# Index key gathers in pairs behind row conversions, and small 32-column products joined to page visits, in a one-core decoder-layer kernel

## The chip, the cores and the metric

The kernel runs on one core of a Trainium2 chip. The metric is the device time of one execution in microseconds (us), lower is better. The engines are TensorE (PE, with its weight loads as PEld), VectorE (DVE), ScalarE (ACT), GpSimd (POOL) and SyncE (SP), which issues most transfers. Each engine works through its own instructions in the order in which they were written; semaphores hold it back until its inputs are there.

## What is computed

One layer of a hybrid decoder, for 256 prompt tokens and 8 requests of 8 new tokens each (320 columns in all), with three groups of heads that read the same projection:

```
z = x @ w_in                        # 2048 -> 8272, split among the three groups
A: I[t,s] = sum_h w[t,h] relu(q_idx[t,h] . k_idx[s])   # 16 index heads x 64
   keep the top 256 (prompt: 64) keys of each query, softmax attention over them
   # 8 heads x 128; keys of the new tokens' requests: 16 pages x 128 past keys + 8 new
B: f = lb + (1-lb) sigmoid(bf);  S_t = diag(f_t) S_{t-1} + (1-f_t) outer i_t
   o_t = S_t^T q_t                  # 4 heads, RMSNorm per head
M: attention into 256 memory tokens # 4 heads
y = LayerNorm(alpha*x + [A*silu, B*silu, M*silu] @ w_out)
```

The keys and values of the past lie in pages of 128 keys that a page table names. The index keys too: `cache_idx_k[page_table]`.

## The kernel before

All products are done in float32 quality. A weight block of 1024 columns comes into `wr`, ACT casts each half to a rounded part `wh`, DVE or POOL subtracts to get the remainder `wl`, and PE multiplies three times (`xh*wh`, `xl*wh`, `xh*wl`). These projection matmuls write `pj`, 48 to a block of 128 output columns, and are most of PE's work. Rotary embedding and evacuation of `pj` are DVE's, POOL's and ACT's.

The order on each engine is fixed when the program is built. A class `Plan` keeps an estimated clock for each engine and an estimated time at which each tile is ready. The main loop issues, at the planned time, either a quantum of projection matmuls (6 of them) or a page unit; around each it resumes the generators in the list `bg` (`background`). A generator yields `need(tiles, ps=n)`: it goes on when the planned clock has passed the tiles' planned times and `n` PSUM banks are free. On the chip nothing of these times is left, only the order.

The parts that matter here:
- **Page units** (`unit`, `units_now`). K units (scores of past keys), V units (their values), XK and XV units (memory of the requests). In these the stationary operand has 32 columns, so four products stand side by side in the array; the trace prints their form as `128*32`. K and V units run in twos where the pages of both are there. A K unit writes half of the bank `kv`, a V unit adds to the bank `va`.
- **Index keys** (`idx_load`). For the four pairs of requests in turn, 16 gathers by POOL fetch the index keys, 128 columns each, into one tile of 2048 columns; their row numbers come from the integer table `poff`.
- **Sample index scores** (`idx_sample`). Twenty steps; in each, `stack` splits 512 (or 8) gathered keys of two requests into rounded part and remainder with ACT and DVE (tile `cat1`), PE takes a group of four score matmuls with the queries (`bp`; the trace says `mA<-cat,bp` or `mB<-cat,bp`), and ACT or DVE applies relu into a ring of four slots of `cat0`. After every second step the head sum (`sums`, matmuls `va<-cat,t`, 32-column form) weighs the heads and is copied or added into the score row `sc` by DVE. The last sums are followed by `topk_sample`: 32 rounds of maximum and replacement on DVE over 1032 scores, then a mask (`maskb`).
- **Prompt index scores** (`idx_prompt`). For each of eight head pairs, four small matmuls once the rotated query `IQ[i]` has been added up, by DVE or POOL, whichever the plan thinks is earlier (`TT`).
- **Sample softmax** (`soft(p)`). Scores of the new tokens (`kv<-akS,qpad`, 32-column form), then mask products (`mA/mB<-maskb,emat`), softmax and transposes for the V units.
- **HGRN** (`hgrn`). For each of four heads a long chain; one piece of it is the product of queries and state (`mA/mB<-bp,t`, 32-column form, 8 matmuls).

## Time and profile before

| | us |
|---|---|
| median of three runs | 907.29 (902.79, 907.29, 907.40) |
| profiled execution | 904.91 |
| its span | 903.2 |
| PE busy | 880.1 (97%) |
| DVE busy | 574.8 (64%) |
| ACT busy | 415.2 (46%) |
| POOL busy | 333.4 (37%) |
| mean granted TensorE clock | 0.996 of full speed |

The profile was taken from one execution. A line gives the start of an instruction from the start of the span, its duration, the engine, the line in the code (nearly all instructions are issued by one helper and have line 142), what it writes and reads, and its form; `x8` is a run of eight alike. In brackets stands how long the engine had been idle, and what ended that. PE's matmuls overlap, so the step from one start to the next tells more than a duration. Plain float32 matmuls run in two passes and count twice.

### The profile page before, as it was taken

The numbers are of one execution on the slowest core, as the hardware profiler recorded it, in microseconds if no ns is written. First come the engines' busy times: TensorE is split into PE (matmuls) and PEld (weight loads), VectorE is DVE, ScalarE is ACT, GpSimd is POOL, SyncE is SP. The second block draws the span as 40 slices with busy tenths as digits, with TensorE's granted clock in tenths as the row PEclk, the third lists the DMA queues.
The fourth block names the chain that finished last, engine by engine and source line by source line (L and its number), as shares of the span: only waits on it lengthen the run. The fifth ranks groups of instructions, "written<-read, shape, count | busy, mean of one in ns | idle before, by whom it ended". The sixth has DMA issues, their size and how long they took to land.

```text
span 903.2 us, 18928 instructions
## 1 busy us (share of the span) xinstructions
PE 880.1 (97%) x6615; PEld 738.9 (82%) x6618; DVE 574.8 (64%) x1191; ACT 415.2 (46%) x872; POOL 333.4 (37%) x322
## 2 busy tenths in 40 slices
PE   8999999999999999999999999999999999999995
PEld 7888877898899888788978787877799788788885
DVE  6677998777689973566654653567544332663656
ACT  6434756654454354334364343434455343554432
POOL 0577774236645530252531441253330001133425
PEclk9999999999999999999999999999999999999998
DMA  8555444499899978999999999999974999856532
GB/s 301 159 167 164 149 115 128 140 402 411 326 409 339 388 277 290 393 353 354 386 378 410 375 404 360 406 352 382 376 290 136 377 409 411 320 168 202 190 94 116
DMA packets 80273, 266.62 MB, mean 295 GB/s; under 512 B 10097, under 2 KB 16946, under 8 KB 79538
## 3 DMA queue, kind: packets, MB, share of 16 engines
q1 hardware_dynamic: 78130, 261.22, 78.2%
q0 software_dynamic: 2048, 4.20, 1.6%
q8 instruction: 52, 0.85, 0.4%
q14 instruction: 43, 0.35, 0.1%
HBM read 256.65 MB, written 8.73 MB: 294 GB/s over the span
## 4 chain that ended last, share of the span: by engine, by line
PE 85%; DVE 10%; DMA 2%; issue 1%; ACT 1%; SPq 0%; POOL 0%; ACTq 0%; DVEq 0%; POOLq 0%
PE pj L142 48%; PE mB L142 12%; PE mA L142 9%; PE va L142 9%; PE kv L142 6%; DVE PT L142 4%; DVE t L142 2%; DVE wl L142 1%; DVE cat L142 1%; DMA wr<-in_wt 1%; DMA pg<-in_xT 1%; ACT wh L142 1%; SPq L142 0%; DVE pg L142 0%; ACT cat L142 0%
## 5 line engine op out<-in xcount | busy, mean ns | idle before, releaser
L142 PE MATMUL pj<-xh,wh 128*128 128x320 f32 x1008 | 324.6, 322 | 1.3 <-ACT t L142 0.9
L142 DVE TENSOR_TENSOR wl<-wr,wh 128x512 fp32r<-128x512 f32 x239 | 186.7, 791 | 212.7 <-ACT wh L142 188.7
L142 PE MATMUL pj<-xh,wl 128*128 128x320 f32 x1008 | 311.0, 309 | 0.8 <-POOL wl L142 0.8
L142 PE MATMUL pj<-xl,wh 128*128 128x320 f32 x1008 | 311.0, 309 | 0.0
L142 ACT CAST wh<-wr 128x512 fp32r<-128x512 f32 x338 | 204.2, 618 | 219.8 <-PE pj L142 170.1
L142 POOL TENSOR_TENSOR wl<-wr,wh 128x512 fp32r<-128x512 f32 x99 | 131.8, 1337 | 334.9 <-ACT wh L142 310.7
L142 PEld LDWEIGHTS pj<-xh,wh 128*128 128x128 f32 x1008 | 189.3, 188 | 28.7 <-issue 22.5
L142 PEld LDWEIGHTS pj<-xl,wh 128*128 128x128 f32 x1008 | 189.4, 188 | 1.2
L142 PEld LDWEIGHTS pj<-xh,wl 128*128 128x128 f32 x1008 | 189.1, 188 | 1.1 <-POOL wl L142 1.1
L142 POOL TENSOR_TENSOR t<-t,t 128x256 fp32r<-128x256 f32 (+4 forms) x69 | 55.6, 807 | 126.2 <-ACT t L142 77.5
L142 ACT ACTIVATE t<-t 128x320 f32<-128x320 f32 (+1 forms) x68 | 29.3, 454 | 66.9 <-DVE t L142 66.2
L142 PE MATMUL kv<-pg,qpad 128*32 128x256 f32 x1024 | 59.8, 381 | 0.0
L142 PE MATMUL va<-pg,PT 128*32 128x512 f32 x512 | 58.7, 596 | 0.0
L142 PEld LDWEIGHTS kv<-pg,qpad 128*32 128x32 f32 x1024 | 31.0, 110 | 21.8 <-issue 1.9
L142 PEld LDWEIGHTS va<-pg,PT 128*32 128x32 f32 x512 | 14.8, 109 | 30.8 <-issue 28.9
L142 DVE MAX8 PT<-PT 128x8 f32<-128x1032 f32 x32 | 39.4, 1232 | 0.5
L142 DVE MATCH_REPLACE8 PT<-PT 128x1032 f32<-128x1032 f32 x32 | 39.0, 1218 | 0.0
L142 POOL DMA_INDIRECT pg<-in_ci,poff x32 | 34.4, 1075 | 11.8 <-issue 8.7
L142 DVE TENSOR_TENSOR t<-t,t 128x320 f32<-128x320 f32 (+4 forms) x55 | 23.0, 418 | 21.9 <-ACT t L142 15.7
L142 POOL DMA_INDIRECT S<-in_ci,poff x32 | 33.4, 1045 | 9.0 <-issue 8.4
L142 POOL TENSOR_TENSOR t<-t,tabm 128x320 f32<-128x320 f32 x16 | 14.0, 876 | 43.6 <-DVE t L142 38.4
L142 PE MATMUL mA<-t,t 128*128 128x64 f32 (+6 forms) x172 | 26.3, 300 | 2.8 <-POOL t L142 2.8
(321 smaller groups left out, 1288.8 us busy)
## 6 DMA issues: line engine op xcount, KB each, us to landing
pg<-in_ck SPq DMA_DIRECT2D x128, 512.0 KB
pg<-in_cv SPq DMA_DIRECT2D x128, 512.0 KB
wr<-in_wt SPq DMA_DIRECT2D x126, 512.0 KB
wr<-in_wo SPq DMA_DIRECT2D x36, 512.0 KB
wr<-in_wm SPq DMA_DIRECT2D x16, 512.0 KB
pg<-in_cXK SPq DMA_DIRECT2D x8, 512.0 KB
pg<-in_cXV SPq DMA_DIRECT2D x8, 512.0 KB
pg<-in_xT SPq DMA_DIRECT2D x8, 320.0 KB
```

Source lines behind the costliest of these rows:

```text
L142: res = f(*a, **k)
```

## The change

- `idx_load` no longer uses an integer table. For each two gathers, DVE converts two columns of row numbers to integers (`row`, a ring of four small tiles), and POOL issues the two gathers that read them. Pairs are at least `PACE` = 2.4 us apart in the plan. The gathers go in the order in which the steps use them, alternating between the two tiles of a side (`sp`), and each quarter of a tile is known by its own planned time.
- `idx_sample` gets a second buffer for relu results (`more`, a page buffer), so that it holds eight slots of 512 and eight of 8, and sums heads four steps at once: four stretches of sums where there were ten. First sums are copied by ACT, not DVE. Score groups need `LAG2` = 0.4 us of planned distance from their inputs, prompt score groups `LAG` = 1.5 us.
- The scores of the new tokens leave `soft` for a generator `new_keys` of their own, and use a bank of the general kind. It and HGRN's query-state product are marked `visit=True`: they wait, for up to `VISIT_WAIT` = 9 us of the plan, until a page unit has been issued, and are then issued right behind it (`join_visit`).
- The two XK units share a bank and go together, as do the two XV units.

In the order on PE, this is the place of the first head sums, before:

```order
L142 MATMUL mA_1273<-cat_4_85,bp_1048 128x512
L142 MATMUL mA_1273<-cat_4_85,bp_1049 128x512
L142 MATMUL mA_1274<-cat_4_85,bp_1048 128x512
L142 MATMUL mA_1274<-cat_4_85,bp_1049 128x512
L142 MATMUL va_1279<-cat_3_84,t_371 32x512 x4
L142 MATMUL pj_1240<-xh,wh_1184 128x320
```

and after, on the same engine (`cat_3` and `pg_1101` are the two buffers of relu results, `t` the head weights):

```order
L146 MATMUL mB_1424<-cat_4_84,bp_1097 128x512
L146 MATMUL mB_1424<-cat_4_84,bp_1098 128x512
L146 MATMUL mB_1425<-cat_4_84,bp_1097 128x512
L146 MATMUL mB_1425<-cat_4_84,bp_1098 128x512
L146 MATMUL va_1430<-cat_3_83,t_372 32x512 x3
L146 MATMUL va_1430<-pg_1101,t_372 32x512 x4
L146 MATMUL va_1430<-cat_3_83,t_372 32x512
L146 MATMUL pj_1391<-xh,wh_1331 128x320
```

Two head sums of four matmuls each have become one stretch of eight, behind the fourth step of scores and not behind the second.

On PE again, the first head's query-state product before (`bp` holds the state, `vN` and `kN` are HGRN's values and keys):

```order
L142 MATMUL kv_5794<-pg_5589,qpad_368 32x256 x2
L142 MATMUL mA_5851<-vN_5196,kN_5784 128x128 x2
L142 MATMUL pj_5718<-xh,wh_5691 128x320
L142 MATMUL pj_5718<-xl,wh_5691 128x320
L142 MATMUL pj_5718<-xh,wl_5692 128x320
L142 MATMUL pj_5718<-xh,wh_5691 128x320
L142 MATMUL pj_5718<-xl,wh_5691 128x320
L142 MATMUL pj_5718<-xh,wl_5692 128x320
L142 MATMUL mB_5885<-bp_5173,t_5000 32x128 x8
L142 MATMUL mB_5894<-t_5171,vN_5196 128x128 x2
```

and after:

```order
L146 MATMUL kv_5898<-pg_5658,qpad_369 32x256 x2
L146 MATMUL kv_5898<-pg_5708,qpad_369 32x256 x2
L146 MATMUL mB_5932<-bp_5165,t_5062 32x128 x8
L146 MATMUL mA_5941<-t_5163,vN_5179 128x128 x2
L146 MATMUL mA_5941<-t_5062,t_5853 128x128
```

The product had a stretch of its own between two pieces of work in full width; now it stands right behind a K unit.

On POOL, the gathers around the first addition of a rotated query (`t<-t,t`), before:

```order
L142 DMA pg_361<-in_ci,poff 128x128 x6
L142 TENSOR_TENSOR t_554<-t_550,t_549 128x256
L142 DMA pg_361<-in_ci,poff 128x128 x8
L142 DMA S_686<-in_ci,poff 128x128 x2
L142 TENSOR_TENSOR t_749<-t_745,t_744 128x256
```

and after:

```order
L146 DMA pg_359<-in_ci,row_446 128x128 x2
L146 DMA S_360<-in_ci,row_491 128x128 x2
L146 DMA S_360<-in_ci,row_523 128x128 x2
L146 TENSOR_TENSOR t_561<-t_557,t_556 128x256
L146 DMA pg_359<-in_ci,row_583 128x128 x2
L146 DMA pg_359<-in_ci,row_615 128x128 x2
```

Each two gathers now read a `row` tile of their own that DVE writes, and the two tiles of a side fill together.

The diff, cut to its core:

```diff
@@ -32,10 +32,14 @@
...
 RES = 7
+PACE = 2.4
 HOMES = 5
...
 SOON = 0.4
+LAG = 1.5
+LAG2 = 0.4
+VISIT_WAIT = 9.0
 TABLES = {AF.Exp: "exp_ln", AF.Ln: "exp_ln", AF.Silu: "silu", AF.Sqrt: "sqrt"}
@@ -205,8 +209,9 @@
...
 
-def need(*aps, ps=1):
-    return (aps, ps)
+def need(*aps, ps=1, lag=0.0, visit=False):
+    return (aps, ps, lag, visit)
 
@@ -672,22 +670,26 @@
...
                               start=False, stop=True)
-                bg.insert(0, [extract(p), ((VACC[p],), 0)])
+                bg.insert(0, [extract(p), need(VACC[p], ps=0)])
                 done.add(("vdone", p))
         elif kind == "XK":
-            ps = PS([128, 256], "kv")
+            if p == 0:
+                st["xk"] = PS([128, 512], "kv")
+            ps = st["xk"][:, 256 * p:256 * p + 256]
             for h in range(4):
...
                               tl[b // 2][:, b % 2, 256 * h:256 * h + 256], start=h == 0, stop=h == 3)
-            bg.insert(0, [xsoft(p, ps), ((ps,), 0)])
+            if p == 1:
+                for g in range(2):
+                    bg.insert(0, [xsoft(g, st["xk"][:, 256 * g:256 * g + 256]), need(st["xk"], ps=0)])
         else:
-            va = PS([128, 512], "va")
+            va = PS([128, 512], ("va", "kv")[p])
             for nt in range(2):
...
                               tl[b // 2][:, b % 2, 512 * nt:512 * nt + 512], start=nt == 0, stop=nt == 1)
-            bg.insert(0, [xextract(p, va), ((va,), 0)])
+            bg.insert(0, [xextract(p, va), need(va, ps=0)])
             if p == 1:
@@ -717,10 +719,12 @@
...
         kind, p, u = punits[n]
-        if kind[0] == "X" or u % 2:
+        if u % 2 or kind[0] == "X" and p:
             return 1
-        if loaded(n + 1) and (kind == "K" or u < 6 or "attn" in done):
+        if loaded(n + 1) and (kind != "V" or u < 6 or "attn" in done):
             return 2
+        if kind[0] == "X":
+            return 0
         if since[0] is None:
@@ -751,16 +755,27 @@
...
     def idx_load():
-        for p in range(4):
-            st["ci", p] = t = new([128, PAST], ("pg", "S")[[0, 1, 0, 1][p]])
-            plan.split.add(t.tensor.name)
-            for j in range(16):
-                if j % 2 == 0:
-                    yield from idle("POOL", 1.5)
-                POOL.indirect_dma_start(out=t[:, 128 * j:128 * j + 128], out_offset=None, in_=I["ci"],
-                                        in_offset=bass.IndirectOffsetOnAxis(ap=poff[:, 16 * p + j:16 * p + j + 1],
-                                                                            axis=0))
-            done.add(("ci", p))
+        t = -9.0
+        for sp in range(2):
+            for p in (2 * sp, 2 * sp + 1):
+                st["ci", p] = x = new([128, PAST], ("pg", "S")[p % 2])
+                plan.split.add(x.tensor.name)
+            for c in range(2):
+                for f in (1, 0):
+                    for p in (2 * sp, 2 * sp + 1):
+                        for j in range(8 * f + 4 * c, 8 * f + 4 * c + 4, 2):
+                            while plan.now < t + PACE:
+                                yield
+                            yield from idle("POOL", 1.5)
+                            t = plan.now
+                            row = new([128, 2], "row", I32)
+                            DVE.tensor_copy(row, st["rows"][:, 16 * p + j:16 * p + j + 2])
+                            for i in range(2):
+                                x = st["ci", p][:, 128 * (j + i):128 * (j + i) + 128]
+                                POOL.indirect_dma_start(out=x, out_offset=None, in_=I["ci"],
+                                                        in_offset=bass.IndirectOffsetOnAxis(ap=row[:, i:i + 1], axis=0))
+                        st["gathered", p, c, f] = x
 
@@ -819,29 +834,44 @@
...
                  for a in range(2)]
-
-        def sums(sp, c, f, r):
-            n = r[0].shape[-1]
-            if f == 1:
-                st["scp"] = PS([128, 512], "va")
-            for g in range(4):
-                PE.matmul(st["scp"][32 * g:32 * g + 32, 0:n], wpad[sp][:, g, f, :], r[g],
-                          start=f == 1, stop=f == 0 or c == 2)
-            if f == 0 or c == 2:
+        more = new([128, 2048], "pg")
+        plan.split.add(more.tensor.name)
+        st["more"] = 1
+        slots = [t[:, 512 * i:512 * i + 512] for t in (early, more) for i in range(4)]
+        small = [early[:, 2784 + 8 * i:2792 + 8 * i] for i in range(8)]
+        used = [0, 0]
+        def relu_slot(n):
+            ring = slots if n > 8 else small
+            used[n > 8] += 1
+            return ring[used[n > 8] % 8][:, 0:n]
+        def sums(sp, rs):
+            for c in sorted({c for c, f in rs}):
+                n = rs[c, 1][0].shape[-1]
+                ps = PS([128, 512], "va") if c < 2 else PS([128, 8])
+                for f in (1, 0) if c < 2 else (1,):
+                    for g in range(4):
+                        PE.matmul(ps[32 * g:32 * g + 32, 0:n], wpad[sp][:, g, f, :], rs[c, f][g],
+                                  start=f == 1, stop=f == 0 or c == 2)
                 d = sc[:, 512 * c:512 * c + n]
-                if sp == 0:
-                    DVE.tensor_copy(d, st["scp"][:, 0:n])
+                if sp:
+                    DVE.tensor_add(d, d, ps[:, 0:n])
+                elif c < 2:
+                    ACT.copy(d, ps[:, 0:n])
                 else:
-                    DVE.tensor_add(d, d, st["scp"][:, 0:n])
+                    DVE.tensor_add(d, ps, tail8)
 
...
                 n, raw = 512, st["ci", 2 * sp + a][:, 1024 * f + 512 * c:1024 * f + 512 * c + 512]
+                kk = [stacked[:, 512 * (2 * (k % 2) + j):512 * (2 * (k % 2) + j) + n] for j in range(2)]
             else:
                 n, raw = 8, st["nk", sp][:, 8 * a:8 * a + 8]
-            kk = [stacked[:, 512 * (2 * (k % 2) + j):512 * (2 * (k % 2) + j) + n] for j in range(2)]
+                kk = [stacked[:, 2048 + 8 * (4 * sp + 2 * a + j):2056 + 8 * (4 * sp + 2 * a + j)] for j in range(2)]
             for j in range(2):
@@ -851,38 +881,44 @@
...
         def keys_in(k):
-            return k >= len(steps) or steps[k][1] == 2 or ("ci", 2 * steps[k][0] + steps[k][3]) in done
+            if k >= len(steps) or steps[k][1] == 2:
+                return True
+            sp, c, f, a = steps[k]
+            x = st.get(("gathered", 2 * sp + a, c, f))
+            return x is not None and plan.avail(x) <= plan.now
 
...
             yield
-        yield need(st["ci", 0])
         kk = stack(0)
-        prev = None
+        rs, full = {}, None
         for k, (sp, c, f, a) in enumerate(steps):
             n = kk[0].shape[-1]
-            yield need(ql, qh, *kk, ps=2)
+            yield need(ql, qh, *kk, ps=2, lag=LAG2)
             pd = [PS([128, 512]), PS([128, 512])]
...
                 PE.matmul(pd[j][:, 0:n], qlr[:, b], kk[j], start=False, stop=True)
-            if a == 0 and k:
-                sums(*prev)
-            r = [relu_slot(n), relu_slot(n)]
-            ACT.activation(r[0], pd[0][:, 0:n], AF.Relu)
-            if plan.t["ACT"] < plan.t["DVE"] + 0.5:
-                ACT.activation(r[1], pd[1][:, 0:n], AF.Relu)
-            else:
-                DVE.tensor_scalar(r[1], pd[1][:, 0:n], 0.0, None, op0=OP.max)
-            prev = (sp, c, f, r if a == 0 else prev[3] + r)
+            if full:
+                sums(*full)
+                full = None
+            r = rs.setdefault((c, f), [])
+            for j in range(2):
+                r.append(relu_slot(n))
+                if j == 0 or plan.t["ACT"] < plan.t["DVE"] + 0.5:
+                    ACT.activation(r[-1], pd[j][:, 0:n], AF.Relu)
+                else:
+                    DVE.tensor_scalar(r[-1], pd[j][:, 0:n], 0.0, None, op0=OP.max)
+            if a == 1 and (c, f) in ((0, 0), (2, 1)):
+                full, rs = (sp, rs), {}
             while not keys_in(k + 1):
...
                 yield
-        yield need(*prev[3], ps=0)
-        sums(*prev)
-        DVE.tensor_add(sc[:, 1024:1032], sc[:, 1024:1032], tail8)
+        yield need(*[x for r in full[1].values() for x in r], ps=1)
+        sums(*full)
+        del st["more"]
         free(ql, qh, *st.pop("wpad"))
@@ -931,7 +967,7 @@
...
             yield from wait(("iq", i))
-            yield need(IQ[i], ik, ps=2)
+            yield need(IQ[i], ik, ps=2, lag=LAG)
             d = [PS([128, 384]), PS([128, 384])]
@@ -1028,23 +1064,28 @@
...
 
-    def soft(p):
-        yield from wait(("K", p), "topk", ("ak", 7), "masks")
-        yield need(akS, st["qpad"], ps=0)
-        while "kv" in st or plan.slot_free("kv", 1) > plan.now:
+    def new_keys(p):
+        yield from wait(("ak", 7))
+        while p not in S:
             yield
-        Sp = S[p]
-        ps = PS([128, NS], "kv")
+        yield need(akS, st["qpad"], visit=True)
+        ps = PS([128, NS])
         for hh in range(2):
...
                               stop=hh == h2 == 1)
-        ACT.activation(Sp[:, PAST:], ps, AF.Copy, scale=QS)
+        ACT.activation(S[p][:, PAST:], ps, AF.Copy, scale=QS)
+        done.add(("new", p))
+    def soft(p):
+        yield from wait(("K", p), ("new", p), "topk", "masks")
+        Sp = S[p]
         mx, rs = T8(), new([128, 4], "s8")
         for i in range(4):
-            yield need(maskb)
+            yield need(maskb, ps=2)
             ps = PS([128, 512])
@@ -1302,7 +1343,7 @@
...
             oT, sq = T(), T()
-            yield need(S1, q, at, S0, ps=2)
+            yield need(S1, q, at, S0, ps=2, visit=True)
             ps = PS([128, 2, 128])
@@ -1733,19 +1773,33 @@
...
                 if e[1]:
-                    deps, nps = e[1]
-                    if any(plan.avail(a) > plan.now for a in deps):
+                    if not met(e[1]):
                         break
-                    if nps:
-                        if n_free("mA") + n_free("mB") < nps:
-                            break
-                try:
-                    e[1] = next(e[0])
-                except StopIteration:
-                    bg.remove(e)
+                    if e[1][3] and nunit < len(punits) and plan.now < asked.setdefault(e[0], plan.now) + VISIT_WAIT:
+                        break
+                if not resume(e) or e[1] is None:
                     break
-                if e[1] is None:
-                    break
+    asked = {}
+    def met(want):
+        deps, nps, lag, _ = want
+        return all(plan.avail(a) + lag <= plan.now for a in deps) and (not nps or n_free("mA") + n_free("mB") >= nps)
+    def resume(e):
+        asked.pop(e[0], None)
+        try:
+            e[1] = next(e[0])
+        except StopIteration:
+            bg.remove(e)
+            return False
+        return True
+    def join_visit():
+        for e in list(bg):
+            if e[1] and e[1][3] and met(e[1]):
+                resume(e)
 
@@ -1766,7 +1820,7 @@
...
             n, b = divmod(npg, 2)
-            if (half > 46 and n < len(punits) and len(PG) + ("q" in st) + ci_live(0) < BUFS["pg"] and n <= nunit + 2
+            if (half > 46 and n < len(punits) and len(PG) + ("q" in st) + ("more" in st) + ci_live(0) < BUFS["pg"] and n <= nunit + 2
                     and plan.slot_free("pg", BUFS["pg"]) <= plan.now + 0.2 and plan.t["DMA"] < plan.now + 8):
@@ -1825,6 +1879,7 @@
...
                 nunit += 1
+            join_visit()
             since[0] = None
```

## Rows read from the trace of the kernel before

**Rows 1.** The page: busy time by engine, and gigabytes per second in 40 slices.
```profile
PE 880.1 (97%) x6615; PEld 738.9 (82%) x6618; DVE 574.8 (64%) x1191; ACT 415.2 (46%) x872; POOL 333.4 (37%) x322
GB/s 301 159 167 164 149 115 128 140 402 411 326 409 339 388 277 290 393 353 354 386 378 410 375 404 360 406 352 382 376 290 136 377 409 411 320 168 202 190 94 116
```
**Rows 2.** PE's waits, first and last of 16: total us, times, longest us.
```profile
PE mA L142 <- POOL t L142: 2.8, 2, 2.2
...
PE pj L142 <- DVE pg L142: 0.2, 1, 0.2
```
**Rows 3.** Timeline of PE around a double K unit: start us, duration us.
```profile
191.89 0.31 PE L142 MATMUL pj<-xh,wl 128*128 128x320 f32 x1
...
192.33 0.31 PE L142 MATMUL pj<-xh,wl 128*128 128x320 f32 x1
192.57 3.66 PE L142 MATMUL kv<-pg,qpad 128*32 128x256 f32 x64
196.16 0.41 PE L142 MATMUL pj<-xh,wh 128*128 128x320 f32 x1
196.41 0.31 PE L142 MATMUL pj<-xl,wh 128*128 128x320 f32 x1
```
**Rows 4.** Timeline of PE around a single K unit.
```profile
207.89 1.93 PE L142 MATMUL kv<-pg,qpad 128*32 128x256 f32 x32
209.76 0.41 PE L142 MATMUL pj<-xh,wh 128*128 128x320 f32 x1
```
**Rows 5.** Timeline of PE at the first head sum.
```profile
104.28 1.07 PE L142 MATMUL va<-cat,t 128*32 128x512 f32 x8
105.28 0.41 PE L142 MATMUL pj<-xh,wh 128*128 128x320 f32 x1
```
**Rows 6.** Timeline of PE at a sample score group with no sum behind it.
```profile
92.61 1.09 PE L142 MATMUL mB<-cat,bp 128*128 128x512 f32 x4
93.53 0.30 PE L142 MATMUL pj<-xh,wh 128*128 128x320 f32 x1
```
**Rows 7.** Timeline of PE at sample score groups that waited, first and last.
```profile
106.99 0.31 PE L142 MATMUL pj<-xh,wl 128*128 128x320 f32 x1
107.72 1.46 PE L142 MATMUL mB<-cat,bp 128*128 128x512 f32 x4 [0.42 <-issue]
109.01 0.31 PE L142 MATMUL pj<-xh,wh 128*128 128x320 f32 x1
...
157.20 1.45 PE L142 MATMUL mA<-cat,bp 128*128 128x512 f32 x4 [0.42 <-DVE cat L142]
```
**Rows 8.** Timeline of PE at prompt score groups that waited, first and last of three.
```profile
46.01 0.93 PE L142 MATMUL mA<-t,t 64*128 64x128 f32 x8 [2.18 <-POOL t L142]
...
80.04 0.93 PE L142 MATMUL mA<-t,t 64*128 64x128 f32 x8 [0.65 <-POOL t L142]
```
**Rows 9.** Timeline of PE at two mask products.
```profile
324.82 0.38 PE L142 MATMUL mB<-maskb,emat 128*128 128x512 bf16 x1 [0.36 <-DVE maskb L142]
...
651.92 0.38 PE L142 MATMUL mB<-maskb,emat 128*128 128x512 bf16 x1 [1.11 <-ACT t L142]
```
**Rows 10.** Timeline of POOL: the last gather before an addition, and the addition.
```profile
40.25 0.94 POOL L142 DMA_INDIRECT pg<-in_ci,poff  x1 [0.30 <-issue]
45.20 0.75 POOL L142 TENSOR_TENSOR t<-t,t 128x256 f32<-128x256 f32 x1 [4.01 <-DVE t L142]
```
**Rows 11.** Busy us in three stretches: PE, PEld, DVE, ACT, POOL; clock, DMA share, GB/s.
```profile
22.00:192.00 170.00, 162.88 (x1071) 142.67 (x1072) 135.04 (x323) 89.57 (x177) 96.28 (x104) 1.00 0.52 163
186.50:324.80 138.30, 137.96 (x1285) 121.96 (x1285) 115.91 (x190) 64.54 (x153) 72.90 (x60) 1.00 0.98 377
346.00:780.00 434.00, 430.92 (x3489) 349.71 (x3490) 230.87 (x509) 186.68 (x404) 112.83 (x118) 1.00 0.94 359
```
**Rows 12.** Timeline of DVE in the sample top-k.
```profile
195.16 1.35 DVE L142 TENSOR_TENSOR wl<-wr,wh 128x512 fp32r<-128x512 f32 x1 [2.88 <-ACT wh L142]
196.43 0.15 DVE L142 RECIPROCAL s<-s 128x2 f32<-128x2 f32 x1
```

More of the change, by code (lines that the diff above doesn't have):

```diff
@@ L306, in hymba_step @@
     pidx = const([128, 64], "pidx", I32)
-    poff = const([128, 64], "poff", I32)
     tabi = [T(), T()]
@@ L705, in unit_ready @@
         if kind == "XK":
[L706 to L708 removed]
+            return p or ("mq", 3) in done and "kv" not in st and plan.slot_free("kv", 1) <= plan.now
+        return p or ("attn" in done and all(("xsoft", g) in done and plan.avail(st["xpt", g]) <= plan.now for g in (0, 1))
+                     and max(plan.slot_free("va", 1), plan.slot_free("kv", 1)) <= plan.now)
     since = [None]
@@ L1677, in setup @@
         DVE.tensor_scalar(pf, pidx, 64.0, dcol[:, 0:1], op0=OP.mult, op1=OP.add)
-        DVE.tensor_copy(poff, pf)
-        free(pf)
+        st["rows"] = pf
         bg.insert(0, [idx_load(), None])
```

15 lines of the change are left out of this document (4 added, 11 removed).

## Prediction

> **What bounds the kernel now.** I read the page first [rows 1]. TensorE (PE) is busy for 880.1 of 903.2 us, 97%; VectorE (DVE) is at 64%. So the time is PE's time, and a gain must be one on PE. The profiled execution took 904.91 us, so 1.7 us lie around its span. A busy PE can still lose time in two ways, and the reader should look for both: it can stand still, and it can work at a worse pace.
>
> The view of PE's waits shows the first: sixteen rows that add up to 13.1 us [rows 2]. The timeline shows the second. A projection matmul (`pj`) starts every 0.147 us while the array stays in one shape (191.89 to 192.33 are three steps) [rows 3]. A stretch of matmuls in 128x32 tiles, which I call a visit, costs more than its matmuls. A visit of 64 passes takes 3.59 us from its first start to the next `pj` (192.57 to 196.16) [rows 3], and one of 32 passes takes 1.87 us (207.89 to 209.76) [rows 4]. So 32 passes more cost 1.72 us, and 0.15 us of every visit belongs to no pass. On top, the first 32-column start comes 0.24 us after the last `pj` start (192.33 to 192.57) and not 0.147, which is 0.09 more, and the `pj` after the visit needs 0.25 us (196.16 to 196.41), 0.10 more. **One visit costs 0.34 us beyond its matmuls.** A head sum shows the same: its eight passes take 1.00 us (104.28 to 105.28) [rows 5], where a score pair without a sum behind it passes into `pj` after 0.92 us (92.61 to 93.53) [rows 6].
>
> Transfers are the next candidate. From 346 to 780 us the DMA engines are 94% busy at 359 GB/s [rows 11], but slices reach 411 GB/s [rows 1] and PE's waits name no transfer.
>
> **The change, part by part.** Each matmul of the kernel is there before and after, with the same sizes. What changes is the order on PE, what stands in front of the gathers, and where small results land.
>
> *Fewer visits.* Counting stretches of 32-row outputs in the two orders gives 61 before and 45 after. Head sums go from 10 to 4, scores of the new tokens from 4 visits of their own to 1 (the other two join a K visit), state products from 4 to none (all join a page visit), the memory pages from 3 to 2, the K pages from 22 to 19, and the V pages from 18 to 19. That is 16 visits less, at 0.34 us each: **-5.4 us**. All of it lies on PE, which has nothing to hide it behind, so it is gained in full if nothing new stops PE. Bounds: 4.2 us (16 x 0.26, if a visit that ends in plain float32 work saves the 0.10 of the following `pj` only sometimes) to 5.6 us.
> On the tile shape the Trainium skill has a rule: the page TensorEngine Tiling (Array Packing), section Key Properties, says that changing the tiling mode, not merely the tile, drains the TensorE. With the drain of 128 cycles that the page TensorE: Matmul & The Clock Gate (section Step-by-step: what each phase is for) gives, two drains at 2.4 GHz are an estimate of 0.11 us a visit, and 16 visits would give 1.7 us; the rows show 0.34 us a visit, and I go by the rows.
>
> *Prompt index scores.* Three of the eight score groups wait 2.18, 0.87 and 0.65 us for an addition on GpSimd (POOL) (first and last in [rows 8]). These are the three whose addition was put there; each stands 30 `pj` matmuls behind the end of its projection. In the new order the two that still have their addition on POOL stand 42 behind it, because 1.5 us of lag are now asked for. Twelve matmuls are 12 x 0.147 = 1.76 us, so 2.18 becomes 0.42 and the others go: **-3.3 us** of 3.7. POOL's additions could come later than now, because two pairs of gathers ahead of them wait for their conversions on DVE. In the trace POOL had been done with its gathers 4.01 us before the addition could start [rows 10], and a pair takes 2 x (0.94 + 0.30) = 2.5 us; this cover is as long as the last pair plus 1.5 us. Range: 1.5 to 3.7 us.
>
> *Sample index scores.* Of the twenty groups, seven follow only 12 `pj` matmuls after the last, and five of these stall or run just behind a stall: 107.72, 126.68, 130.43, 133.97, 157.20. The first starts 0.73 us after the `pj` ahead of it and not 0.147, and lasts 1.29 us (107.72 to 109.01) against 0.92 [rows 6, 7]: 0.95 us lost. Worked out alike, the five cost 0.95 + 1.29 + 0.83 + 0.20 + 0.94 = 4.2 us (of the first and the last the rows stand). Of the thirteen others, 18 matmuls or more behind the last, one stalls, at 147.84, for a weight half. In the new order none follows after fewer than 18, and most after 24. I take **-4.0 us**; range 1.5 to 4.2, since stacks and sums are differently spread.
>
> *Masks of the sample softmax.* The first mask product waits 0.36 us for the top-k and the one at 651.92 waits 1.11 us for a bank that ScalarE (ACT) still reads [rows 9]; before each, new-token scores had just been done. The new order does those long before and asks for two free banks. I take **-0.8 us**, half; range 0 to -1.6.
>
> *Conversions and gathers.* There are 32 small DVE instructions more. The nearest row is a 128x2 reciprocal of 0.15 us [rows 12]: 32 x 0.15 = 4.8 us at most. DVE is idle for 170.0 - 135.0 = 35 us between 22 and 192 us [rows 11], so it has room. The wait is the doubtful part. From the fifth on, a conversion waits until the pair of gathers four places ahead has landed, and behind it in DVE's queue stand weight remainders (`wl`) and rotary work that empties `pj`. Four pairs are 4 x 2.5 = 10 us of POOL's time, so the pair should have landed. I allow **+1.5 us** for new stalls of any kind; bounds 0 and 17 us (the rival below).
> The gathers now alternate between two requests and end later, and the last head sums stand 83 rows later on PE, with one K visit ahead of them. That moves the top-k: on PE the way from the last sums to the first mask product shrinks by 30 `pj` (4.4 us), one double visit (3.4 us) and three visits' cost (1.0 us), less about 1.0 us of work that comes in, so from 138.3 [rows 11] to some 130 us. DVE is busy for 115.9 us of it. By the order, two rotary evictions, three `wl` and a few small ones leave the chain, about 3.6 us. More important, blocked stretches go: four of the five `wl` in the chain of before wait 2.9 us each (the first in [rows 12]), and the chain of after has two `wl`. 115.9 - 3.6 = 112 us must fit into 130; I count nothing.
> State products and X products wait for a page visit, up to 9 us of the planner's time; the four HGRN heads end long before the tail, whose order on PE is the same but for a few transposes. I count nothing.
>
> **The sum.** 904.9 - 5.4 - 3.3 - 4.0 - 0.8 + 1.5 = 892.9. The three runs of before are 902.79, 907.29 and 907.4 us, so the profiled one lies between the lowest and the median; I correct nothing. **893 us.**
>
> **The rivals.**
> *The stalls only move.* The order is made for planned durations, and a new order meets new errors; the 13.1 us of waits are such errors now. If as much is lost in other places, only the visits count: 904.9 - 5.4 = 899.5. For it: the sample scores have more work packed ahead of their first sums. Against it: where visits are long and spaced, PE loses only 434.0 - 430.9 = 3.1 us in 434 [rows 11].
> *The top-k comes late.* If DVE's chain shortened by its 3.6 us alone and kept its idle stretches, PE would come 8 - 3.6 = 4.4 us too early at the first mask product: 892.9 + 4.4 = 897.3. Against it: the idle stretches belong to instructions that left the chain. This lies in the forecast's range.
> *Slower: DVE held up by the gathers.* 28 conversions wait for a pair of gathers, POOL's queue holds rotary work that waits for DVE in turn, and behind each conversion stand the `wl` halves that PE needs. The four halves kept ready cover 4 x 12 x 0.147 = 7 us, so single delays are hidden; repeated ones are not. PE loses 28 times the mean excess: 0.43 us each eats the 12 us, and at 0.6 us each the time is 892.9 - 1.5 + 17 = 908. For it: POOL is busy 96 of 170 us there [rows 11], and a gather is at times longer than 0.94 us. Against it: the 10 us above.
> *The change does not do what it says.* A visit's price could lie not in the change of shape but in the work next to it, and a joined visit would then pay it inside. The two visits of 32 and 64 passes say no, since the second unit of a double visit costs 1.72 us and not 1.87; new banks are the one difference. Then 892.9 + 5.4 = 898.
>
> **How the numbers follow.** Forecast, 887 to 898 (with the late top-k): 0.72. Stalls only move, 899.5, between 898 and 902: 0.16. No gain from the joins: 0.05, at 898. DVE held up, 908: 0.07. A measurement of this kernel tells about 0.5% (4.5 us) from no change; by the median of before the bound is 902.8, by the profiled run 900.4. The first and third cases lie under both, the second one at the bound, so I give it two thirds. Faster 0.72 + 0.05 + 0.10 = 0.87, less 0.03 for runs that differ among themselves: 0.84; same 0.10; slower 0.06. The range leaves out the slow rival and the best end: 886 to 902.
>
> **What would show it.** In the profile after, PE busy time falls by about 5 us and its waits from 13 to about 6. The waits for `POOL t` are under 1 us together, and no sample score group lasts over 1.2 us. State products follow a page visit without `pj` between. A head sum's eight passes and the next eight come as one stretch of 1.86 us. DVE shows no wait above 1 us at a conversion. Wrong would be: waits of PE for `wl` in 22 to 192 us of more than 3 us (conversions); a wait at the first mask product over 2 us (top-k); a single visit that no longer costs 0.34 us; waits that name pages.

## The result, and the profile after

The changed kernel takes 893.86 us (median of four runs, 892.59 to 896.41) against 905.56 us for the kernel before (four runs, 902.79 to 907.4): a ratio of 0.9877, with a 95% interval from 0.9838 to 0.9915. The prediction was 893.0 us, 886 to 902, faster.

The profiled execution has a span of 891.9 us, 11.3 us less than before. The page of the kernel after, first part, answers [rows 1]:

```profile
PE 873.6 (98%) x6616; PEld 741.9 (83%) x6618; DVE 578.3 (65%) x1211; ACT 416.9 (47%) x873; POOL 347.6 (39%) x331
```

PE is busy 6.5 us less, and is still the engine that sets the time. PE's waits after, all of them (total us, times, longest us), answer [rows 2]:

```profile
PE pj L146 <- ACT t L146: 2.0, 2, 1.4
PE mB L146 <- DVE maskb L146: 1.5, 1, 1.5
PE mA L146 <- DVE cat L146: 1.4, 1, 1.4
PE kv L1692 <- DVE t L146: 1.1, 1, 1.1
PE mB L146 <- issue: 0.7, 2, 0.5
PE mB L146 <- DVE wl L146: 0.6, 1, 0.6
PE pj L146 <- issue: 0.4, 1, 0.4
PE pj L146 <- DVE xl L146: 0.3, 1, 0.3
PE mA L146 <- POOL t L146: 0.2, 1, 0.2
PE pj L146 <- DVE pg L146: 0.2, 1, 0.2
PE pj L146 <- ACT qpad L146: 0.2, 1, 0.2
PE mA L146 <- issue: 0.2, 1, 0.2
```

They add up to 8.8 us, 4.3 less than before. The row for `POOL t`, once 2.8 and 0.9, is down to 0.2; the mask's row has grown from 0.4 to 1.5. The timeline of PE after shows the places: the one prompt group that still waits, a sample group of 8 columns, and the mask products that answer [rows 9]:

```profile
79.31 0.93 PE L146 MATMUL mA<-t,t 64*128 64x128 f32 x8 [0.20 <-POOL t L146]
...
135.87 0.61 PE L146 MATMUL mA<-cat,bp 128*128 128x8 f32 x4 [1.38 <-DVE cat L146]
...
325.37 0.39 PE L146 MATMUL mB<-maskb,emat 128*128 128x512 bf16 x1 [1.48 <-DVE maskb L146]
...
653.88 0.38 PE L146 MATMUL mA<-maskb,emat 128*128 128x512 bf16 x1 [0.16 <-issue]
```

The joins are there. In the timeline of PE after, the query-state product (`mB<-bp,t`) starts with no `pj` between, 3.48 us after the start of a double K unit:

```profile
405.26 0.31 PE L146 MATMUL pj<-xh,wl 128*128 128x320 f32 x1
405.50 3.66 PE L146 MATMUL kv<-pg,qpad 128*32 128x256 f32 x64
408.98 0.62 PE L146 MATMUL mB<-bp,t 128*32 128x128 f32 x16
409.52 0.71 PE L146 MATMUL mA<-t,vN 128*128 128x128 f32 x4
```

Counted in the traces, stretches in 128x32 form are 61 before and 45 after. The conversions never left DVE waiting, though their 7.8 us are more than the 4.8 us that the working gave as an upper bound; this is their group after (total us, mean ns, idle us before them):

```profile
L146 DVE CAST row<-rows 128x2 int32<-128x2 f32 x32 | 7.8, 243 | 0.2
```

### The profile page after: what moved, and what is told of

It reads as the page before. It is cut to its first block, busy times and chain, and to the rows that moved or that the text cites. A ratio compares the mean times of both kernels' runs of the same rounds, so it can differ in the third digit from the quotient of the medians.

```text
span 891.9 us, 19000 instructions
## 1 busy us (share of the span) xinstructions
PE 873.6 (98%) x6616; PEld 741.9 (83%) x6618; DVE 578.3 (65%) x1211; ACT 416.9 (47%) x873; POOL 347.6 (39%) x331
## 5 line engine op out<-in xcount | busy, mean ns | idle before, releaser
L146 DVE TENSOR_TENSOR wl<-wr,wh 128x512 fp32r<-128x512 f32 x232 | 175.8, 768 | 175.5 <-ACT wh L146 163.6
L146 POOL TENSOR_TENSOR wl<-wr,wh 128x512 fp32r<-128x512 f32 x106 | 142.9, 1352 | 299.9 <-ACT wh L146 277.9
L146 POOL TENSOR_TENSOR t<-t,t 128x320 f32<-128x320 f32 (+4 forms) x71 | 57.3, 808 | 142.6 <-DVE t L146 72.8
L146 POOL DMA_INDIRECT pg<-in_ci,row x32 | 34.1, 1065 | 23.2 <-DVE row L146 13.0
L146 POOL DMA_INDIRECT S<-in_ci,row x32 | 34.7, 1084 | 18.2 <-issue 7.9
L146 DVE TENSOR_TENSOR t<-t,t 128x128 f32<-128x128 f32 (+5 forms) x53 | 22.3, 420 | 17.6 <-ACT t L146 15.2
L146 POOL TENSOR_TENSOR t<-t 128x256 f32<-128x256 f32 (+2 forms) x28 | 23.5, 843 | 5.1 <-DVE t L146 5.1
L146 ACT ACTIVATE S<-kv 128x512 f32<-128x512 f32 x16 | 9.6, 599 | 31.9 <-PE kv L146 31.9
```

The lines of the kernel that those rows point to most:

```text
L146: res = f(*a, **k)
```

## The experiments

Comparisons were made on several chips, and the kernel before is not equally fast on them: about 905.5 us where the result was measured and in two of the four comparisons below, about 899.1 us in the other two. Each measurement is given with the time of the kernel before beside it; this difference turned out to be a part of the answer.

### The price of a visit: the same small groups inside a visit, alone, and in full shape

Four matmuls on zero columns (eight passes) are issued 26 times, either inside a page visit or one quantum ahead of it. The edit; the call ahead of the quantum is that of the run with the groups alone, the last one that of the run with the groups inside:

```diff
+    def more_work(n):
+        if primed[n] and extras[0] < 36:
+            ps, c, first = primed[n]
+            for g in range(0, 128, 32):
+                nc.tensor.matmul(ps[g:g + 32, c:c + 64], ident[:, g:g + 32], zero, start=first, stop=first)
...
                 open_bank(nunit)
+                more_work(nunit)
                 pe_quantum(half, quarter)
...
             if nunit in primed:
+                more_work(nunit)
```

In the third run the call is ahead of the quantum too, and the loop reads `nc.tensor.matmul(ps[:, c:c + 64], ident, zero, ...)`, four times.

> The changed kernel with 26 extra groups of four tiny matmuls (128x32 stationary, 64 zero columns, eight passes), each inside a page visit, at its start; before each page visit one quantum of projection is put in, so that the next run can differ in the place of the groups alone. 47 visits. Both theories: 26 x 8 passes x 0.02 us = 4.2 us of matmuls on top of the changed kernel's 893.9 us, so about 898, with PE's steps at a visit as before.

> The same kernel and the same 26 groups, but each group stands six projection matmuls (or one other quantum) ahead of its visit, as a visit of its own: 73 visits. Theory (a visit costs 0.34 us beyond its matmuls): 26 x 0.34 = 8.8 us longer than the run with the groups inside, about 907. Rival (the price is in the work next to it, a change of shape costs nothing): the same time as with the groups inside, within 1.5 us. An estimate by the drain that the Trainium skill's page TensorE: Matmul & The Clock Gate (section Step-by-step: what each phase is for) gives, two a visit: 26 x 0.11 = 2.8 us longer.

> The groups stand where they stand in the run with the groups alone, but each is four matmuls of a full 128x128 stationary on the same 64 zero columns: plain float32 still, no change of the array's shape, 47 visits. Theory (the shape is what costs): no late first start (0.15 us after the last projection start and not 0.24); a plain float32 matmul in full shape takes about 0.2 us for its two passes, so the groups themselves take 26 x 0.8 = 21 us. Rival (the change from rounded to plain float32 costs, not the shape): the first start is 0.24 us late here too, and the projection matmul behind needs 0.25 us.

Measured beside the kernel before at 899.23 us: inside 897.62 us (ratio 0.9978, 0.9969 to 0.9988), alone 904.58 us (1.0057, 1.0040 to 1.0073), full shape 914.54 us (one run). A visit of its own thus costs 904.58 - 897.62 = 6.96 us for 26, 0.27 us each. The timelines of PE show what it consists of. First the run with the group inside, then alone, then in full shape:

```profile
194.77 0.31 PE L146 MATMUL pj<-xh,wl 128*128 128x320 f32 x1
195.01 0.32 PE L655 MATMUL kv<-zero,ident 128*32 128x64 f32 x8
195.15 3.64 PE L146 MATMUL kv<-pg,qpad 128*32 128x256 f32 x64
```

```profile
196.19 0.31 PE L146 MATMUL pj<-xh,wl 128*128 128x320 f32 x1
196.43 0.32 PE L655 MATMUL kv<-zero,ident 128*32 128x64 f32 x8
196.68 0.42 PE L146 MATMUL pj<-xh,wh 128*128 128x320 f32 x1
196.94 0.31 PE L146 MATMUL pj<-xl,wh 128*128 128x320 f32 x1
```

```profile
195.13 0.31 PE L146 MATMUL pj<-xh,wl 128*128 128x320 f32 x1
195.28 1.00 PE L655 MATMUL kv<-zero,ident 128*128 128x64 f32 x8
196.08 0.39 PE L146 MATMUL pj<-xh,wh 128*128 128x320 f32 x1
196.31 0.31 PE L146 MATMUL pj<-xl,wh 128*128 128x320 f32 x1
```

Inside, the group takes 0.14 us (195.01 to 195.15). Alone, from the start of the last `pj` to the second `pj` behind it, 0.75 us pass (196.19 to 196.94), where two plain steps would be 0.29. That is 0.46 us for a group of 0.14: **0.31 us is the visit's own**, in 18 of the 26 places to within 0.01. The other eight stand beside work in other forms. The whole runs cannot say whether these pay less: their intervals allow 0.20 to 0.33 us for the mean of 26, and runs of equal mean granted clock (0.996 to 0.997) give 0.29 (903.7 and 904.0 us alone, 895.9 to 896.4 us inside). The price has three pieces: 0.09 at the entry (0.24 for 0.147), 0.11 in the stretch (0.25 until the next `pj` for 0.14), and 0.11 at the first `pj` behind (0.26 for 0.147). In full shape the entry is free (195.13 to 195.28 is a plain step), but the `pj` behind is still late, by 0.08 (0.23). So the late entry, 0.09 us, belongs to the change of shape, and most of the last piece to the change between plain float32 and rounded parts, as the rival had it for all of the price. The 0.11 us in the stretch cannot be assigned by these rows, since in full shape the eight passes themselves take longer (0.80 us, 195.28 to 196.08). That a joined matmul pays the same inside its visit is refuted.

### All joins and sums taken back

```diff
-        yield need(akS, st["qpad"], visit=True)
+        yield need(akS, st["qpad"])
...
-            yield need(S1, q, at, S0, ps=2, visit=True)
+            yield need(S1, q, at, S0, ps=2)
...
-            if a == 1 and (c, f) in ((0, 0), (2, 1)):
+            if a == 1:
```

(`sums` then handles one pair of steps at a time.)

> The changed kernel with the joins taken back: new-token scores and state products no longer wait for a page visit, and head sums come after every second step and not every fourth. Lags, gathers and conversions stay. 55 visits and not 45. Theory: 10 x 0.34 = 3.4 us longer than the changed kernel, about 897.3, give or take 2 us for stalls that move. Rival (only the stalls counted): 893.9, no difference.

Measured 900.19 us beside 899.23 (1.0014, 1.0004 to 1.0023). The changed kernel took 891.61 beside 899.08 on another chip where before is that fast (below), so the undoing costs 8.6 us and not 3.4. The traces of the two say where. Ten visits at 0.31 are 3.1 us. PE's waits are 2.4 us longer; the largest is one behind which the clock fell. Timeline, then windows (busy us of PE, PEld, DVE, ACT, POOL; granted clock, DMA share, GB/s) of the run with the joins undone:

```profile
646.55 0.64 PE L146 MATMUL pj<-xh,wh 128*128 128x320 f32 x1 [2.94 <-ACT t L146]
646.99 0.47 PE L146 MATMUL pj<-xl,wh 128*128 128x320 f32 x1
647.25 0.47 PE L146 MATMUL pj<-xh,wl 128*128 128x320 f32 x1
```

```profile
630.00:646.00 16.00, 13.61 (x127) 10.30 (x126) 12.03 (x27) 6.58 (x11) 5.60 (x6) 1.00 1.00 388
646.00:650.00 4.00, 3.45 (x14) 3.45 (x15) 0.77 (x2) 2.36 (x8) 1.27 (x1) 0.57 1.00 380
650.00:666.00 16.00, 16.00 (x114) 15.88 (x114) 6.24 (x11) 7.39 (x19) 4.97 (x4) 1.00 0.68 236
```

PE stood still for 2.94 us, and behind that a `pj` step is 0.26 us (646.99 to 647.25) and not 0.147: most of these 4 us lie at the lower of the clock's two levels. The changed kernel waits 1.41 us at this place, and its clock stays at the upper one. The slow stretch costs up to 4 x (1 - 0.57) = 1.7 us more; of the 8.5 us between the spans, 1.3 stay without a name. The theory's size fits the visits (55 stretches are counted in this trace); what it left out is that a new order moves stalls, and that the clock fell behind one of them.

### The changed kernel again, its lags set to zero, and the lags alone

```diff
-LAG = 1.5
-LAG2 = 0.4
+LAG = 0.0
+LAG2 = 0.0
```

The run with the lags alone is the kernel before with `lag=LAG` and `lag=LAG2` at the two `need` lines of the score groups.

> The changed kernel once more, beside the variants of this call. By the prediction's sum: 12 us less than before, ratio 0.987. If its gain is smaller on this chip, the difference between chips is told from the trace.

> The changed kernel with both lags at zero, all else as it is. In its order the prompt score groups stand 30 projection matmuls behind the end of their projection again, as before, and three sample groups follow only 12 behind the last (none in the changed kernel, seven before). Theory: the three waits for POOL's addition come back, 3.3 us, and 3 x 0.84 = 2.5 us at the sample groups: 5.8 us longer than the changed kernel. Rival (the packed gathers and the sums of four steps, not the lags, took the stalls away): the same time, within 1.5 us.

> The kernel before with the two lags alone (1.5 us at prompt score groups, 0.4 us at sample groups). Its order has 57 visits and not 61, prompt groups at 42 and not at 30, and two sample groups at 12 and not seven. Theory: 3.3 us for the prompt waits, 5 x 0.84 = 4.2 less a little at the sample groups, 4 x 0.31 = 1.2 us for visits that fell together: about 8 us shorter than before. Rival (stalls only move in a new order): no more than 3 us shorter.

Measured beside the kernel before at 905.61 us: changed again 895.17 us (0.9886, 0.9857 to 0.9915), without lags 896.73 us (0.9902, 0.9883 to 0.9922), lags alone 922.24 us (1.0189, 1.0165 to 1.0212). Both of my theories on the lags fell. Without them only 1.6 us are lost, with overlapping intervals, which is about what the rival had (within 1.5 us). Of the three prompt waits, two came back and the first did not; the timeline of PE without lags, where the kernel before had 2.18, 0.87 and 0.65 ([rows 8] and the prediction):

```profile
43.39 0.93 PE L146 MATMUL mA<-t,t 64*128 64x128 f32 x8 [0.19 <-POOL t L146]
60.50 0.93 PE L146 MATMUL mB<-t,t 64*128 64x128 f32 x8 [0.86 <-POOL t L146]
77.52 0.93 PE L146 MATMUL mA<-t,t 64*128 64x128 f32 x8 [0.77 <-POOL t L146]
```

In the trace of before DVE had reached the rotary work behind the first of these late: a weight remainder ahead of it stood idle for 2.65 us. The profile names no releaser, but ACT's cast of a weight half had ended at 39.52 us, just ahead of it, and by the order of the casts that is the half it reads:

```profile
38.90 0.62 ACT L142 CAST wh<-wr 128x512 fp32r<-128x512 f32 x1 [0.58 <-issue]
39.68 0.69 DVE L142 TENSOR_TENSOR wl<-wr,wh 128x512 fp32r<-128x512 f32 x1 [2.65 <-issue]
```

And the lags alone cost 16.6 us. Their windows show where:

```profile
60.00:76.00 16.00, 15.62 (x108) 14.27 (x107) 12.00 (x33) 6.11 (x12) 10.53 (x10) 1.00 0.52 159
76.00:82.00 6.00, 3.93 (x21) 2.81 (x19) 3.54 (x11) 0.62 (x1) 4.47 (x6) 1.00 0.27 69
82.00:90.00 8.00, 3.44 (x10) 2.43 (x11) 1.90 (x6) 0.62 (x1) 6.17 (x7) 0.54 0.38 118
90.00:97.00 7.00, 4.04 (x12) 3.09 (x12) 0.73 (x2) 1.38 (x3) 2.23 (x3) 0.50 0.09 28
```

From 76 to 97 us PE is busy for only 11.4 of 21 us, DVE for 6.2 and ACT for 2.6; the DMA engines are busy for 9 to 38%, and from 82 us on the granted clock is about half, the lower of its two levels. In this order POOL issues 22 gathers with nothing between them (63.9 to 92.8 us); the kernel before has no such row of more than ten, because an addition that waits for DVE stands between. Neither expectation had this; whether the row of gathers is the cause is what the next runs test.

The changed kernel is not free of it either. Its six runs here take 893.3 to 901.4 us, and the trace is of the longest: at the end of a row of ten gathers (68.4 to 81.7 us) PE stands without a releaser, first for 0.95 us, and from 83.6 to 87.1 us the granted clock is 0.51:

```profile
81.55 0.30 PE L146 MATMUL pj<-xh,wl 128*128 128x320 f32 x1 [0.95 <-issue]
```

### Without the conversions, with and without gaps between the gathers

The gathers of the changed kernel read the integer table of before, in the new order; then the same with memsets on POOL behind every eighth gather, which change no other engine's order:

```diff
-                            row = new([128, 2], "row", I32)
-                            DVE.tensor_copy(row, st["rows"][:, 16 * p + j:16 * p + j + 2])
...
-ap=row[:, i:i + 1]
+ap=poff[:, 16 * p + j + i:16 * p + j + i + 1]
...
+                    for i in range(18):
+                        nc.gpsimd.memset(filler, 0.0)
```

> The changed kernel without the conversions on DVE: the gathers read one integer table as before, in the new order and at the new pace. Theory: conversions cost PE nothing, so the same as the changed kernel within 1.5 us, apart from one sample group that stands 12 behind the last (0.8 us longer). Rival (the conversions hold DVE and POOL up): shorter by 2 us or more, with POOL's waits for the rows gone. Rival the other way (the conversions are what spaces the gathers to advantage): longer by 3 us or more.

> The changed kernel a third time, because the kernel before took 905.6 us in two of the comparisons so far and 899.2 in another, in whose traces DVE, ACT and PE show almost no idle time that ends without a semaphore (0.2 us in 22 to 192 us, against 6.5 on DVE in the trace of before). Theory A (part of the gain of 12 us was that the new order suffers less from such idle time while gathers run): where the kernel before takes about 899, the gain is 5 to 7 us and no such idle time shows; where it takes about 905, the gain is 10 to 12. Rival B (the gain does not depend on it): 11 to 12 us in either case.

> The variant without conversions (gathers read the integer table; 911.5 us against the changed kernel's 895.2), with its orders unchanged but for 18 small memsets on POOL after every eighth gather, about 3 us in which POOL issues none. Theory (20 gathers back to back keep the other engines from being served; the conversions broke such rows up): the idle time without a semaphore on PE, DVE and ACT at 77 to 95 us goes, and the time comes back to 895 or 898. Rival (the conversions matter in another way, by the instructions that moved with them): it stays near 911. Where the kernel before takes about 899, neither can be told from the other.

> The variant without conversions once more, beside its copy with gaps. Theory (20 gathers back to back leave the other engines unserved, but only on some chips: where the kernel before takes about 905 and not 899): where before takes about 899, this takes 896 to 899, within 2 us of the copy with gaps measured there (897.5), PE has no idle time without a semaphore at 57 to 93 us and the granted clock stays at full there. Where before takes about 905, it takes 908 to 914, as it did. Rival (the order alone costs the 16 us): 908 or more on either.

> Its copy with about 3 us of memsets on POOL behind every eighth gather. Theory: where before takes about 905, the gaps take most of the 16 us away (895 to 901), and the half-speed stretch of the clock at 84 us goes; where it takes about 899, the same as without gaps within 2 us. Rival: no difference from the variant without gaps on either.

| beside the kernel before at | changed | without conversions | without them, with gaps |
|---|---|---|---|
| 905.61 us | 895.17 (0.9886, 0.9857 to 0.9915) | 911.48 (1.0065, 1.0044 to 1.0087) | |
| 905.41 us | | 912.68 (1.0079, 1.0050 to 1.0107) | 898.38 (0.9921, 0.9892 to 0.9949) |
| 899.08 us | 891.61 (0.9920, 0.9907 to 0.9933) | | 897.54 (0.9985, 0.9975 to 0.9995) |

Taking the conversions out costs 16.3 us (911.48 - 895.17), and gaps between the gathers take 14.3 us away (912.68 - 898.38), on one chip and with the same order on every other engine. So most of what the conversions do for the time there is to break the rows of gathers up: in the trace of the result POOL waits for them ten times, 20.1 us in all. Not all: where the kernel before takes 899.1 us, the copy with gaps shows no idle time of PE without a releaser between 22 and 192 us and is still 5.9 us longer than the changed kernel (897.54 against 891.61). Its order and the gaps differ from the changed kernel's, and no run separates these two. The timeline of PE without conversions, beside the kernel before at 905.41 us, in the row of 20 gathers that began at 65.44 us:

```profile
80.02 0.31 PE L146 MATMUL pj<-xh,wl 128*128 128x320 f32 x1 [0.34 <-issue]
81.45 0.30 PE L146 MATMUL pj<-xh,wh 128*128 128x320 f32 x1 [0.69 <-issue]
...
85.09 0.37 PE L146 MATMUL mA<-t,t 64*128 64x128 f32 x1 [1.14 <-issue]
...
94.30 0.76 PE L146 MATMUL mA<-t,t 64*128 64x256 f32 x1 [0.64 <-issue]
```

`<-issue` says that PE waited for nothing that the profile shows. The last two rows are the first and the last pass of a prompt score group, whose eight take 0.93 us in [rows 8]; here they take 10 us (85.09 to 95.06), far more than a granted clock of half would make of them. DVE stands for 10.46 us with the same mark, but that is no stall of its own: by the order of the casts, the remainder that it starts at 94.34 us reads the half that ACT casts until 93.51 us. ACT had stood for 12.23 us before that cast. The profile puts this down to a prompt score matmul, but in the copy with gaps the same cast starts at 75.35 us, before the first of these matmuls (78.91 us), so it does not need them. POOL's gathers meanwhile go on at their own pace, one in 1.25 us:

```profile
92.89 0.62 ACT L146 CAST wh<-wr 128x512 fp32r<-128x512 f32 x1 [12.23 <-PE mA L146]
94.34 2.01 DVE L146 TENSOR_TENSOR wl<-wr,wh 128x512 fp32r<-128x512 f32 x3 [10.46 <-issue]
```

```profile
87.93 0.94 POOL L146 DMA_INDIRECT pg<-in_ci,poff  x1 [0.30 <-issue]
89.18 0.94 POOL L146 DMA_INDIRECT S<-in_ci,poff  x1 [0.30 <-issue]
```

Windows of the same stretch, first without gaps, then with gaps on the same chip:

```profile
77.00:98.00 21.00, 11.64 (x45) 8.73 (x44) 8.43 (x22) 3.19 (x7) 11.02 (x12) 0.68 0.31 89
```

```profile
77.00:98.00 21.00, 20.69 (x139) 19.15 (x138) 18.49 (x44) 12.25 (x22) 16.10 (x31) 1.00 0.55 163
```

PE is busy for 9 us less without gaps, and the lower granted clock (0.68 on the mean of 21 us) can cost up to another 6.7 us; together that is 15.8 of the 17.4 us between the two spans (912.1 and 894.7 us).

The third run of the changed kernel shows that chips matter: where the kernel before takes 899.1 us, the gain is 7.5 us, a little above the 5 to 7 of theory A and far from the 11 to 12 of rival B. There, DVE has 0.2 us of idle time without a releaser between 22 and 192 us (6.5 on DVE in the trace of before, 6.7 in the trace of the result). That figure tells the two kinds of chips apart, but not how long DVE waited for nothing, since the traces of the first kind lack records: between 22 and 160 us 157 of DVE's 211 semaphore updates (the signals by which it releases others) are recorded in the trace of before, and all 240 in that of the third run. With gaps DVE still has 5.5 us of such idle time where the kernel before takes 905.4 us, and PE loses 0.3.

The run without conversions was never measured where the kernel before takes 899 us: its second run was on a chip where before takes 905.41 us. So the first half of both expectations for those runs stays untested, and that long rows do no harm on the other kind of chip is not shown.

## Why the prediction was right, point by point

**Where the 11.3 us came from.** The two traces' steps from start to start, grouped by form, divide it: 4.3 us are waits, 2.0 us are sample score groups that ran behind a stall without a wait of their own (the steps of `mA/mB<-cat,bp` add up to 19.45 us before and 17.50 after), and 5.0 us are left by subtraction, as much as 16 visits at 0.31 us.

**Fewer visits.** Predicted -5.4 us at 0.34 a visit; 16 visits at the measured 0.31 are -5.0. The count and the argument held. The price was a little high; the whole runs gave 0.27 to 0.29, above the lower bound of 0.26. For the shape alone the runs show between 0.09 (the late entry) and 0.23 us (all but the 0.08 that full shape pays too). By the drains that the Trainium skill's page TensorE: Matmul & The Clock Gate (section Step-by-step: what each phase is for) states, an estimate is 0.11 us a visit; it lies in that span, and it is a third of the whole price.

**Prompt scores.** Predicted -3.3, measured 3.70 - 0.20 = -3.5. The size was right; the cause only in part. With the lags at zero these waits are 1.8 us and not 3.7, so the lag is worth about half. The other half is the first wait alone, 2.18 us before and 0.19 without lags: there POOL's addition waited for DVE, and DVE for ACT's cast; why that cast came late in the kernel before is not shown.

**Sample scores.** Predicted -4.0, measured -2.7: 2.0 us as said, and waits down from 3.22 to 2.45. The term is mis-sized because I made the distance to the last group the whole cause: the two groups of 8 columns still stall (0.50 and 1.38 us) at 24 and 18 matmuls behind the last, the longer one for DVE's stack (`DVE cat`). Nor is it the lag that spreads the groups: with the lags at zero they lose no more (17.79 us of steps, 1.38 of waits), so the sums of four steps and the new order of gathers do it, and which of the two is not shown.

**Masks.** Predicted -0.8, measured +0.2: the bank's 1.11 us went to 0.16, but the top-k is now late by 1.48 us where it was 0.36. PE's way from the last head sums to the first mask product is 132.4 us (193.00 to 325.37, 1.48 of it waiting), where I had written some 130, and DVE's chain did not get as short: DVE is busy for 114.5 us of it, where I had 112, and idle for 17.9. This is the late top-k inside my forecast, at 1.5 us and not 4.4.

**New stalls.** Allowed +1.5, measured -0.2 for all other places. The allowance was not needed, and it makes up for most of the 2.3 us by which the sample scores and the masks fell short; that the sum came within 1 us is luck to that extent. Two of the signs named in the prediction did not come: PE's waits are 8.8 us and not about 6, and one sample group lasts 1.36 us (110.31 to 111.67), above 1.2.

**The rivals.** That stalls only move is refuted by the 6 us of stalls that went. That a joined visit pays its price inside is refuted by the small groups. That DVE is held up by the gathers did not happen: 0.2 us of idle time ahead of 32 conversions.

**What the working missed.** Its doubtful term, the conversions, was bounded between a cost of 0 and one of 17 us. Where the kernel before takes 905.6 us they are worth 16 us, since the lags remove what broke the gathers' rows in the kernel before: lags alone make it 922. I had set the trace of before against one edit at a time. The nearest rows were there ([rows 10] shows the last gather of a row, and POOL waiting 4.01 us for DVE behind it), but I read that wait as cover and not as a pause that the other engines needed. The number came out since the edits were made together, and as far as the working goes that was luck. It also holds for chips of the kind that the trace of before was taken on: the total contains some 3 to 4 us (11.7 and 10.4 against 7.5) that other chips do not have to give. Which of the terms shrink there is not shown, since no trace of the kernel before was taken on such a chip.

## What to carry to other kernels

Price a change of tile shape as a step of its own, by comparing stretches of different length and the step on each side: here 0.31 us a time, on the engine that sets the end. Before an ordering edit, ask what it takes out from between instructions on every queue, not only what it adds; a wait in one queue can be a pause that the other engines need. And test edits that belong together both together and apart: here the lags alone lose 16.6 us, and the whole gains 10 to 12 on the same kind of chip.

## What the runs showed of the hardware that was not expected

Long rows of gathers issued by POOL hold PE up, and ACT in the stretch followed above, on chips where the kernel before takes about 905.5 us. In four rows of 10 to 22 gathers at one in 1.25 us or a little more, PE's first idle time without a releaser came in the tenth or eleventh gather (57.38 us in a row from 44.3 and 78.53 in one from 63.9, lags alone; 58.94 from 45.9 and 80.02 from 65.4, without conversions), and the last of it ended within 3 us of the row's end. PE then starts a matmul at distances of about 0.72, 1.43 or 2.1 us. The DMA engines are 31% busy at the time, so they are not full. Three rows of ten in the trace of before leave no such time on PE, so ten is not always enough. Where the kernel before takes 899.1 us, the changed kernel has two rows of ten and no such stall. With gaps behind every eighth gather, 0.31 us of it is left on PE.

What is short there stays open. The Trainium skill's page SBUF — State Buffer (section Who interferes with whom) says that DVE and GpSimd share a pair of ports that one of them holds exclusively, and that PE and ACT never wait on anyone; by that rule a lost port cannot be what PE and ACT stood for. Nor do the rows here show one for DVE, whose 10.46 us are a wait for ACT until 93.51 us. The semaphore records that the traces lack lie in the same stretch (22 to 160 us) and on the same chips, and every time on record comes with a span and a granted clock read from a profile, so the runs cannot tell whether the recording takes part in the stall. No run here told chips apart other than by their times and traces, and none varied the size of a gather, which would tell the number of rows fetched from the bytes.
